# Running sums in a pooling mixer, a fifth pair of weight tiles, and weight units prepared three ahead

## The chip, the core and the metric

The kernel runs on one core of a Trainium2 chip. A core has a matmul engine (TensorE, PE in the profile; PEld is its weight load), a vector engine (DVE), a scalar engine (ACT), a general engine (POOL) and a sync engine (SP) that here issues DMAs. Each takes its instructions in order from a queue of its own and waits on semaphores. They share an on-chip memory (SBUF); matmuls write to eight PSUM banks, which DVE and ACT read. The metric is the device time of one execution in microseconds (us).

## The reference, cut to what matters

A two-layer decoder trunk on 512 tokens of 1,024 channels, all in float32. Each layer has a mixer, cross-attention into 256 memory tokens, and a gated feed-forward (FFN) with a short causal convolution, each behind an RMSNorm. Layer 0's mixer is a gated DeltaNet beside a state-space model; layer 1's is the pooling mixer:

```python
POOL_WINDOWS = (2, 4, 8, 16)             # one per group of 256 channels
for gi, win in enumerate(POOL_WINDOWS):
    csg = cs[..., sl]                    # running sum over the tokens
    lower = jnp.pad(csg, ((0, 0), (win, 0), (0, 0)))[:, 1:t + 1]
    mean = (csg[:, 1:] - lower) / jnp.minimum(pos_count, float(win))
    outs.append(jnp.einsum('btc,ce->bte', mean - xf[..., sl], pool_w[gi]))
return jnp.concatenate(outs, axis=-1) * pool_scale
```

The first tokens, which have fewer than `win` tokens behind them, are divided by their own count.

## The kernel before, in words

Activations lie transposed: eight tiles `x[0..7]` of 128 channels by 512 tokens. Every float32 product is three matmuls of a split into a high and a low half (`mm3`, lines 185 to 187): high by high, low by high, high by low.

**Weight units.** All weights come in a list of units of 128 x 1,024 (512 KB, some 128 x 768), in the order in which PE uses them. A unit is loaded by SP into one of three `raw` tiles (`_load`, line 127), ACT casts it to the high half `wh` (line 136), and the low half `wl` is made in one of two ways: DVE subtracts (line 141), or, for the units listed in `pool_units`, ACT writes minus the raw weights (line 138) and POOL has a DMA add the weights from memory on top (line 139). There are four pairs of `wh` and `wl`. `w()` hands out the next unit and, before that, prepares units up to `LOOK` = 2 ahead. So the cast of unit j has to wait until PE is done with unit j-4, and a raw load until the casts of the unit three before are done.

**Order.** PE and SP run in the order of the code. DVE, ACT and POOL are put in order by the framework's scheduler when the program is built, so their queues are fixed in the program but not written in the code.

**The stretch that matters here** begins when the FFN of layer 0 ends. `pool_mixer` multiplies the normalized tiles by the pool weights (two units, eight products `pl`) and keeps PE going with work in the background, `run(bg, 3)`: the values of layer 1 (`values`, two pairs of products `vp`, eight units, each pair read by `vh` on ACT, line 373, and `vl` on DVE, line 374) and the last five keys (`keys`, products `kp`, five units). Every second of these units gets its low half by DMA. Then the query products of the attention follow (`Q`, products `in`, units `wq`), 24 matmuls of 512 columns each. In the built program the first query product has the PSUM bank of the first value product, and the second that of the third.

Meanwhile DVE takes the windows in the order 8, 16, 4, 2. For each it multiplies the two products by the row of norms (line 646), forms the window sums by doubling adds over 2 x 512 columns (line 649: three for window 8, four for 16, two for 4, one for 2), corrects the first columns by count (653), turns sums into mean minus token (657), and adds the scaled result to the two `x` tiles (660). ACT then makes `xh` and the squares of the new tiles (226, 242), DVE `xl` (227).

Of the kernel before, what the change touches and what calls it, by code (L numbers as in the profile page):

```python
# [14 lines left out]
F32R = mybir.dt.float32r  # L15
I32 = mybir.dt.int32
AF = mybir.ActivationFunctionType
ALU = mybir.AluOpType
# [4 lines left out]
KT = D // 128  # L23
# [33 lines left out]
class Net:  # L57
    def __init__(self, tc, A, ctx):
        self.tc, self.nc, self.A = tc, tc.nc, A
        nc = self.nc  # L60
        P = lambda name, bufs, **k: ctx.enter_context(tc.tile_pool(name=name, bufs=bufs, **k))
        self.cp = P("cp", 1)
        self.wp = P("wp", 1)
        self.ap_ = P("ap", 56)
        self.sc = None
        self.tp = P("tp", 8)
        self.zp = P("zp", 4)
        self.rp = P("rp", 2)
        self.dp = P("dp", 4, space=bass.MemoryType.DRAM)
        self.n = 0  # L70
        self.units = []
        self.pool_units = ()
        self.area = None
        self.tset = "n"
        self.prepped = {}
        self.loaded = {}
        self.ui = 0
        self.small = self.cp.tile([128, NSMALL], F32, name="small")
        o, w = SMALL["g_mix"]
        nc.scalar.dma_start(self.small[:, o : o + w], A["small"][:, o : o + w])  # L80
        self.ident = self.cp.tile([128, 128], F32, name="ident")
        make_identity(nc, self.ident)
        self.ones = self.cp.tile([128, 128], F32, name="ones")
        nc.gpsimd.memset(self.ones, 1.0)
# [33 lines left out]


    LOOK = 2  # L120
    PAD = 8

    def _load(self, i):
        if i not in self.loaded:
# [4 lines left out]
    def _prep(self, i):  # L129
        nc = self.nc  # L130
        self._load(i)
        raw = self.loaded[i]
        n = raw.shape[1]
        H = self.wp.tile([128, n], F32R, tag="wh", bufs=4, name=self.nm("wh"))
        L = self.wp.tile([128, n], F32R, tag="wl", bufs=4, name=self.nm("wl"))
        nc.scalar.copy(H, raw)  # L136
        if i in self.pool_units:
            nc.scalar.activation(L, raw, AF.Copy, scale=-1.0)  # L138
            nc.gpsimd.dma_start(L, self.units[i], accum_op=ALU.add)
        else:  # L140
            nc.vector.tensor_tensor(L, raw, H.bitcast(F32), ALU.subtract)  # L141
        self.prepped[i] = (H, L)

    def first(self, N, src):
# [8 lines left out]
        def part(i, p):  # L153
            nc.sync.dma_start(self.loaded[i][:, p], self.units[i][:, p])
            H, L = self.prepped[i]
            nc.scalar.copy(H[:, p], self.loaded[i][:, p])
            nc.vector.tensor_tensor(L[:, p], self.loaded[i][:, p], H[:, p].bitcast(F32), ALU.subtract)

# [452 lines left out]
    def pool_mixer(self, x, N, bg, after):  # L611
        nc = self.nc
        ws = [self.w(), self.w()]

        for t in self.wb:
            nc.gpsimd.memset(t[:, :, : self.PAD], 0.0)

        def mm(m):
            gi, e = m // 2, m % 2
            w = ws[gi // 2]  # L620
            ps = self.psum("pl")
            for kk in range(2):
                o = (gi % 2) * 512 + kk * 256 + e * 128
                self.mm3(ps, (w[0][:, o : o + 128], w[1][:, o : o + 128]), N["hl"][gi * 2 + kk], kk == 0, kk == 1)
            return ps

        pss = {}
        order = (4, 5, 6, 7, 2, 3, 0, 1)
        for i, m in enumerate(order):
            if i == 4:  # L630
                r = self.norm_end(N)
            pss[m] = mm(m)
            if i >= 4:
                z = self.t(F32, "plz")
                nc.scalar.copy(z, pss[m])
                pss[m] = z
        rB = self.row(r, range(4))

        v = nc.vector
        defer = []  # L640
        for gi in (2, 3, 1, 0):
            win = WINDOWS[gi]
            at = lambda t, sh: t[:, :, self.PAD - sh : self.PAD - sh + T]
            z, ping, pong = self.wb
            for e in range(2):
                v.tensor_tensor(at(z, 0)[:, e, :], pss[2 * gi + e], rB, ALU.mult)
            cur, sh = z, 1
            while sh < win:
                v.tensor_tensor(at(ping, 0), at(cur, 0), at(cur, sh), ALU.add)
                cur, ping, pong = ping, pong, ping  # L650
                sh *= 2
            cur = at(cur, 0)
            v.tensor_tensor(cur[:, :, : win - 1], cur[:, :, : win - 1], self.cnt[:, gi : gi + 1, : win - 1].to_broadcast([128, 2, win - 1]), ALU.mult)
            for f in defer:
                f()
            defer = []
            v.scalar_tensor_tensor(cur, cur, 1.0 / win, at(z, 0), ALU.mult, ALU.subtract)
            for e in range(2):
                m = 2 * gi + e
                v.scalar_tensor_tensor(x[m], cur[:, e, :], self.sm("pool_scale", m), x[m], ALU.mult, ALU.add)  # L660
                after(m, defer)
            self.run(bg, 3)
        for f in defer:
            f()
# [786 lines left out]
def trunk(tc, A, out, ctx):  # L1451
    n = Net(tc, A, ctx)
# [5 lines left out]
    b = 0  # L1458
# [29 lines left out]
    psum = dict(space=bass.MemoryType.PSUM)  # L1488
    with tc.tile_pool(name="mp", bufs=1) as n.mp, tc.tile_pool(name="mix", bufs=1) as n.pp, tc.tile_pool(name="ps", bufs=6, **psum) as n.ps, tc.tile_pool(name="px", bufs=1, **psum) as n.px:
# [6 lines left out]
        x = []  # L1496
        hl = n.mixer0(N, kv, x)
        N = n.norm_begin("g_xa", 0)
        for _ in n.proj_residual(x, hl, lambda m: n.norm_tile(N, x[m]), 3, (4, 6, 7, 8)):
            pass  # L1500
    with tc.tile_pool(name="win", bufs=1) as wpool, tc.tile_pool(name="ps8", bufs=8, **psum) as n.ps:
        for l in range(2):
            if l == 1:
                N = n.norm_begin("g_xa", 1)
                bg = chain(n.values(kv[1], kv[2]), kv[3])
                n.wb = [wpool.tile([128, 2, n.PAD + T], F32, name=n.nm("wb")) for _ in range(3)]
                n.pool_mixer(x, Nn, bg, lambda m, q: n.norm_tile(N, x[m], at=m, defer=q))
                n.run(bg)
            Nf = n.norm_begin("g_ffn", l)
            n.attention(x, N, kv, lambda m: n.norm_tile(Nf, x[m]))  # L1510
            Nn = n.norm_begin("g_final", 0) if l else n.norm_begin("g_mix", 1)
            def next_keys():
                kv[:2] = [], []
                kv.append(n.keys(kv[0], kv[2]))
                n.run(kv[3], 6)

            n.ffn(l, x, Nf, None if l else next_keys, (Nn, out) if l else lambda m: n.norm_tile(Nn, x[m]))
# [73 lines left out]
```

## Time and profile before

| | us |
|---|---|
| median of three runs | 1413.93 (1413.61 to 1413.98) |
| the profiled execution | 1411.4 |
| its span, first to last instruction | 1409.6 |
| PE busy in it | 1356.5 (96%) |
| DVE busy | 909.8 (65%) |
| ACT busy | 618.6 (44%) |
| POOL busy | 220.4 (16%) |

An engine's busy share is an average over stages. What decides is PE's idle time: where it lies, and what ended it. The granted clock of PE (PEclk) is a share of full speed. The first 320 us are the mixer of layer 0, the stretch above runs from about 860 to 930.

### The profile page before, as it was taken

How to read it: one execution, taken by the hardware profiler on the slowest of the kernel's cores; microseconds unless marked ns; L12 is line 12 of the kernel's file. 1: busy time of each engine (PE TensorE's matmuls, PEld its weight loads, DVE VectorE, ACT ScalarE, POOL GpSimd, SP SyncE). 2: the span in 40 equal slices, each digit the busy share in tenths (PEclk: the TensorE clock that was granted, in tenths of full speed). 3: DMA queues.
4: the chain of work that ended last, by engine and by line, in shares of the span. 5: the costliest groups of instructions: out<-in, count | busy, mean ns of one | idle time of the engine just before them, and what ended most of it. 6: DMA issues, size and time to landing. Idle time of an engine off the chain costs nothing.

```text
span 1409.6 us, 17658 instructions
## 1 busy us (share of the span) xinstructions
PE 1356.5 (96%) x6699; PEld 1143.3 (81%) x6699; DVE 909.8 (65%) x1552; ACT 618.6 (44%) x948; POOL 220.4 (16%) x350
## 2 busy tenths in 40 slices
PE   8799988999999999999999999899999999999997
PEld 6678878988788888888888888778888888888886
DVE  7967877466645677637754766965657736663764
ACT  6446574545443444324422445654434423432442
POOL 2495827210200200000000002200100000000003
PEclk9789979999999999999999999989999999999999
DMA  7424424453321323332323236932233333323221
GB/s 233 111 90 105 126 43 124 106 179 106 121 73 46 105 90 105 90 105 90 105 90 102 89 109 149 252 84 64 65 97 98 95 100 93 102 77 118 87 69 69
DMA packets 50628, 146.63 MB, mean 104 GB/s; under 512 B 7664, under 2 KB 13936, under 8 KB 50544
## 3 DMA queue, kind: packets, MB, share of 16 engines
q1 hardware_dynamic: 40480, 127.29, 28.6%
q0 software_dynamic: 3744, 13.63, 5.6%
q10 hardware_dynamic: 6320, 4.60, 1.1%
q8 instruction: 52, 0.85, 0.2%
q14 instruction: 32, 0.26, 0.1%
HBM read 141.30 MB, written 4.19 MB: 103 GB/s over the span
## 4 chain that ended last, share of the span: by engine, by line
PE 80%; DVE 6%; POOL 4%; DMA 3%; ACT 3%; issue 2%; ACTq 1%; POOLq 0%; SPq 0%; DVEq 0%
PE in L185 14%; PE in L186 14%; PE in L187 14%; PE op L186 9%; PE op L185 9%; PE op L187 9%; DVE cv L755 1%; ACT wl L138 1%; DMA so<-dy 1%; DMA dy<-sg 1%; PE kp L186 1%; PE kp L187 1%; PE kp L185 1%; DMA wl<-in_wk 1%; PE sc L187 1%
## 5 line engine op out<-in xcount | busy, mean ns | idle before, releaser
L136 ACT CAST wh<-raw 128x1024 fp32r<-128x1024 f32 (+1 forms) x230 | 237.0, 1036 | 399.7 <-PE op L186 148.0
L185 PE MATMUL in<-xh,wh 128*128 128x512 f32 x992 | 392.2, 395 | 13.9 <-DVE vl L374 7.0
L186 PE MATMUL in<-xl,wh 128*128 128x512 f32 x992 | 389.9, 393 | 0.0
L187 PE MATMUL in<-xh,wl 128*128 128x512 f32 x992 | 389.2, 392 | 0.6 <-DVE wl L141 0.6
L141 DVE TENSOR_TENSOR wl<-raw,wh 128x1024 fp32r<-128x1024 f32 (+1 forms) x204 | 246.1, 1209 | 80.2 <-ACT wh L136 77.9
L185 PEld LDWEIGHTS in<-xh,wh 128*128 128x128 f32 x992 | 188.4, 190 | 53.6 <-DVE vl L374 7.2
L187 PEld LDWEIGHTS in<-xh,wl 128*128 128x128 f32 x992 | 188.3, 190 | 40.5 <-DVE wl L141 1.0
L186 PEld LDWEIGHTS in<-xl,wh 128*128 128x128 f32 x992 | 188.4, 190 | 39.2 <-DVE xl L227 1.0
L247 POOL TENSOR_TENSOR sq<-sq,sq 128x512 f32<-128x512 f32 x28 | 46.7, 1669 | 967.9 <-ACT sq L242 869.5
L469 DVE TENSOR_TENSOR x<-op,x 128x512 f32<-128x512 f32 x68 | 46.9, 690 | 151.2 <-PE op L187 151.2
L185 PE MATMUL op<-fh,wh 128*128 128x512 f32 (+1 forms) x376 | 141.4, 376 | 0.0
L186 PE MATMUL op<-fl,wh 128*128 128x512 f32 (+1 forms) x376 | 141.2, 376 | 0.0
L187 PE MATMUL op<-fh,wl 128*128 128x512 f32 (+1 forms) x376 | 141.2, 376 | 0.0
L572 DVE TENSOR_TENSOR h<-in,rB 128x512 f32<-128x512 f32 x88 | 60.2, 688 | 87.1 <-PE in L187 87.1
L185 PEld LDWEIGHTS op<-fh,wh 128*128 128x128 f32 x376 | 70.8, 188 | 12.9
L186 PEld LDWEIGHTS op<-fl,wh 128*128 128x128 f32 x376 | 70.8, 188 | 12.7
L187 PEld LDWEIGHTS op<-fh,wl 128*128 128x128 f32 x376 | 70.8, 188 | 12.7
L192 ACT CAST fh<-a 128x512 fp32r<-128x512 f32 x44 | 27.3, 621 | 110.6 <-DVE a L584 110.6
L576 ACT ACTIVATE a<-h,small 128x512 f32<-128x512 f32 x88 | 63.3, 721 | 10.5 <-DVE h L572 9.8
L578 DVE SCALAR_TENSOR_TENSOR a<-h,small,a 128x510 f32<-128x510 f32 x88 | 65.8, 750 | 2.9
L577 DVE SCALAR_TENSOR_TENSOR a<-h,small,a 128x511 f32<-128x511 f32 x88 | 65.4, 746 | 2.5 <-ACT a L576 2.5
L580 ACT ACTIVATE a<-a 128x512 f32<-128x512 f32 x44 | 27.8, 632 | 81.0 <-DVE a L578 81.0
(460 smaller groups left out, 2111.7 us busy)
## 6 DMA issues: line engine op xcount, KB each, us to landing
raw<-in_up SPq DMA_DIRECT2D x88, 512.0 KB, 3.5
raw<-in_dn SPq DMA_DIRECT2D x32, 512.0 KB, 3.5
raw<-in_w_in SPq DMA_DIRECT2D x18, 512.0 KB, 4.3
raw<-in_wk SPq DMA_DIRECT2D x16, 512.0 KB, 4.4
raw<-in_wv SPq DMA_DIRECT2D x16, 512.0 KB, 3.9
raw<-in_wq SPq DMA_DIRECT2D x16, 512.0 KB, 4.5
raw<-in_wo SPq DMA_DIRECT2D x16, 512.0 KB, 3.5
raw<-in_dn SPq DMA_DIRECT2D x16, 384.0 KB, 2.9
```

The costliest lines, as they stand in the source:

```text
L136: nc.scalar.copy(H, raw)
L141: nc.vector.tensor_tensor(L, raw, H.bitcast(F32), ALU.subtract)
L185: mm(ps, wh, xh, start=start, stop=False)
L186: mm(ps, wh, xl, start=False, stop=False)
L187: mm(ps, wl, xh, start=False, stop=stop)
L247: eng.tensor_tensor(N["acc"], N["acc"], sq, ALU.add)
L469: nc.vector.tensor_tensor(x[m], ps, x[m], ALU.add)
L572: nc.vector.tensor_tensor(h, ps, rB, ALU.mult)
L576: nc.scalar.activation(a, h, AF.Copy, scale=cw(2))
L577: nc.vector.scalar_tensor_tensor(a[:, 1:], h[:, : T - 1], cw(1), a[:, 1:], ALU.mult, ALU.add)
L578: nc.vector.scalar_tensor_tensor(a[:, 2:], h[:, : T - 2], cw(0), a[:, 2:], ALU.mult, ALU.add)
L580: nc.scalar.activation(a, a, AF.Silu)
```

## The change

It has three parts. Window sums: for windows 8 and 16 DVE keeps a running sum with one scan per tile (add the new column, subtract the one `win` back), which needs 16 columns of zeros ahead of the tile (`PAD`); window 4 keeps its two adds; window 2 becomes half of the token before minus the token, with the half put into the scale (`half`, made once). Weights: when the first mixer is over, every fifth unit has a pair of its own in a new pool `wx`, so five pairs rotate. And from there on `LOOK` is 3.

```diff
-    PAD = 8
+    PAD = 16
...
     def _prep(self, i):
...
-        H = self.wp.tile([128, n], F32R, tag="wh", bufs=4, name=self.nm("wh"))
-        L = self.wp.tile([128, n], F32R, tag="wl", bufs=4, name=self.nm("wl"))
+        p, b = (self.wx, 1) if self.wx and i % 5 == 4 else (self.wp, 4)
+        H = p.tile([128, n], F32R, tag="wh", bufs=b, name=self.nm("wh"))
+        L = p.tile([128, n], F32R, tag="wl", bufs=b, name=self.nm("wl"))
...
     def pool_mixer(self, x, N, bg, after):
...
+        half = self.tiny(KT, "half")
+        v.tensor_scalar_mul(half, self.sm("pool_scale", 0, KT), 0.5)
...
-            cur, sh = z, 1
-            while sh < win:
-                v.tensor_tensor(at(ping, 0), at(cur, 0), at(cur, sh), ALU.add)
-                cur, ping, pong = ping, pong, ping
-                sh *= 2
-            cur = at(cur, 0)
-            v.tensor_tensor(cur[:, :, : win - 1], cur[:, :, : win - 1], self.cnt[:, gi : gi + 1, : win - 1].to_broadcast([128, 2, win - 1]), ALU.mult)
+            z0 = at(z, 0)
+            cur = at(ping, 0)
+            scale = lambda m: self.sm("pool_scale", m)
+            if win == 2:
+
+                v.tensor_tensor(cur, at(z, 1), z0, ALU.subtract)
+                v.memset(cur[:, :, 0:1], 0.0)
+                scale = lambda m: half[:, m : m + 1]
+            else:
+                if win == 4:
+                    v.tensor_tensor(at(pong, 0), z0, at(z, 1), ALU.add)
+                    v.tensor_tensor(cur, at(pong, 0), at(pong, 2), ALU.add)
+                else:
+
+                    for e in range(2):
+                        v.tensor_tensor_scan(cur[:, e, :], z0[:, e, :], at(z, win)[:, e, :], 0.0, ALU.add, ALU.subtract)
+                v.tensor_tensor(cur[:, :, : win - 1], cur[:, :, : win - 1], self.cnt[:, gi : gi + 1, : win - 1].to_broadcast([128, 2, win - 1]), ALU.mult)
...
-            v.scalar_tensor_tensor(cur, cur, 1.0 / win, at(z, 0), ALU.mult, ALU.subtract)
+            if win > 2:
+                v.scalar_tensor_tensor(cur, cur, 1.0 / win, z0, ALU.mult, ALU.subtract)
...
-                v.scalar_tensor_tensor(x[m], cur[:, e, :], self.sm("pool_scale", m), x[m], ALU.mult, ALU.add)
+                v.scalar_tensor_tensor(x[m], cur[:, e, :], scale(m), x[m], ALU.mult, ALU.add)
...
-    with tc.tile_pool(name="win", bufs=1) as wpool, tc.tile_pool(name="ps8", bufs=8, **psum) as n.ps:
+    with tc.tile_pool(name="win", bufs=1) as wpool, tc.tile_pool(name="wx", bufs=1) as n.wx, tc.tile_pool(name="ps8", bufs=8, **psum) as n.ps:
+        n.LOOK = 3
```

The orders of PE and SP stay as they were. On ACT, at the end of the background work, the queue before reads (`raw_1503`, `raw_1508`, `raw_1521` are the second, third and fourth query units, `x_583` and `x_584` are tiles 2 and 3 of `x`, `vp_1427` is the first value product):

```order
L136 CAST wh_1504_8015<-raw_1503_8013 128x1024
L138 ACTIVATE wl_1505_8016<-raw_1503_8013 128x1024
L136 CAST wh_1509_8051<-raw_1508_8049 128x1024
L136 CAST wh_1522_8111<-raw_1521_8109 128x1024
L138 ACTIVATE wl_1523_8112<-raw_1521_8109 128x1024
L226 ACTIVATE xh_1444_7723<-x_583_3154,small_75 128x512
L242 ACTIVATE sq_1446_7726<-x_583_3154 128x512
L226 ACTIVATE xh_1447_7730<-x_584_3156,small_75 128x512
L242 ACTIVATE sq_1449_7733<-x_584_3156 128x512
L373 ACTIVATE vh_1453_7754<-vp_1427_7632,r_406_2305 128x512
L373 ACTIVATE vh_1455_7758<-vp_1428_7633,r_406_2305 128x512
```

There the two `vh` are behind the casts of three query units. Now, at the same place on ACT (`raw_1496`, `raw_1500`, `raw_1507`, `raw_1512` are the first to fourth query units, `vp_1431` the first value product; lines are those of the changed code):

```order
L138 CAST wh_1497_7951<-raw_1496_7949 128x1024
L349 CAST kh_1336_7239<-kt_1335_7238 128x256
L228 ACTIVATE xh_1448_7731<-x_583_3154,small_75 128x512
L244 ACTIVATE sq_1450_7734<-x_583_3154 128x512
L228 ACTIVATE xh_1451_7738<-x_584_3156,small_75 128x512
L244 ACTIVATE sq_1453_7741<-x_584_3156 128x512
L375 ACTIVATE vh_1457_7763<-vp_1431_7643,r_406_2305 128x512
L138 CAST wh_1501_7985<-raw_1500_7983 128x1024
L140 ACTIVATE wl_1502_7986<-raw_1500_7983 128x1024
L375 ACTIVATE vh_1459_7767<-vp_1432_7644,r_406_2305 128x512
L138 CAST wh_1508_8023<-raw_1507_8021 128x1024
L138 CAST wh_1513_8058<-raw_1512_8056 128x1024
```

The first `vh` now stands ahead of the second query unit's cast, the second ahead of the third's. A little further on ACT, the `vh` of the second pair of value products (`vp_1461`) stands behind the cast of the fifth query unit (`raw_1525`):

```order
L244 ACTIVATE sq_1468_7795<-x_581_3150 128x512
L140 ACTIVATE wl_1514_8059<-raw_1512_8056 128x1024
L228 ACTIVATE xh_1469_7799<-x_582_3152,small_75 128x512
L244 ACTIVATE sq_1471_7802<-x_582_3152 128x512
L138 CAST wh_1526_8119<-raw_1525_8117 128x1024
L375 ACTIVATE vh_1481_7869<-vp_1461_7771,r_406_2305 128x512
L375 ACTIVATE vh_1483_7873<-vp_1462_7772,r_406_2305 128x512
```

Before, the casts of that unit came after this `vh`. On DVE, the window of 16 read before:

```order
L646 TENSOR_TENSOR wb_1391_7498<-pl_1403_7538,rB_1420_7610 128x512
L227 SCALAR_TENSOR_TENSOR xl_1422_7621<-x_585_3158,small_75,xh_1421_7620 128x512
L649 TENSOR_TENSOR wb_1392_7499<-wb_1391_7498 128x2x512
L141 TENSOR_TENSOR wl_1470_7807<-raw_1468_7804,wh_1469_7806 128x1024
L227 SCALAR_TENSOR_TENSOR xl_1425_7627<-x_586_3160,small_75,xh_1424_7626 128x512
L649 TENSOR_TENSOR wb_1393_7500<-wb_1392_7499 128x2x512
L141 TENSOR_TENSOR wl_1476_7846<-raw_1474_7843,wh_1475_7845 128x1024
L649 TENSOR_TENSOR wb_1392_7499<-wb_1393_7500 128x2x512
L649 TENSOR_TENSOR wb_1393_7500<-wb_1392_7499 128x2x512
L653 TENSOR_TENSOR wb_1393_7500<-wb_1393_7500,cnt_98 128x2x15
```

and now (line 666 is the scan, printed under the name of a like operation, twice in a row):

```order
L650 TENSOR_TENSOR wb_1394_7508<-pl_1406_7548,rB_1423_7620 128x512
L229 SCALAR_TENSOR_TENSOR xl_1426_7632<-x_585_3158,small_75,xh_1425_7631 128x512
L666 SCALAR_TENSOR_TENSOR wb_1395_7509<-wb_1394_7508 128x512 x2
L143 TENSOR_TENSOR wl_1465_7776<-raw_1463_7773,wh_1464_7775 128x1024
L229 SCALAR_TENSOR_TENSOR xl_1429_7638<-x_586_3160,small_75,xh_1428_7637 128x512
L667 TENSOR_TENSOR wb_1395_7509<-wb_1395_7509,cnt_98 128x2x15
```

Four adds have become two scans, and one weight subtract that stood between them has moved behind.

## Rows read from the trace of the kernel before

**Rows 1.** The page, part 1: busy us, share of the span, count.

```profile
PE 1356.5 (96%) x6699; PEld 1143.3 (81%) x6699; DVE 909.8 (65%) x1552; ACT 618.6 (44%) x948; POOL 220.4 (16%) x350
```

**Rows 2.** Windows: length, busy us and count by engine, clock, DMA share, GB/s.

```profile
860.00:920.00 60.00, 50.77 (x278) 43.15 (x277) 48.63 (x66) 36.69 (x47) 14.81 (x13) 0.96 0.87 219
920.00:980.00 60.00, 60.00 (x299) 50.92 (x298) 37.50 (x81) 27.99 (x57) 0.00 (x0) 0.96 0.23 69
```

**Rows 3.** Timeline of PE: start, us, instruction, idle before it and its releaser.

```profile
890.28 0.50 PE L186 MATMUL vp<-wl,mz 128*128 128x512 f32 x1 [0.80 <-DMA wl<-in_wv]
...
896.62 0.39 PE L187 MATMUL kp<-mz,wl 128*128 128x256 f32 x1 [0.46 <-DMA wl<-in_wk]
...
909.20 0.38 PE L187 MATMUL kp<-mz,wl 128*128 128x256 f32 x1 [1.00 <-DMA wl<-in_wk]
...
918.92 0.79 PE L185 MATMUL in<-xh,wh 128*128 128x512 f32 x1 [6.96 <-DVE vl L374]
```

**Rows 4.** Windows within the stretch, columns as in rows 2.

```profile
858.00:872.00 14.00, 14.00 (x66) 11.54 (x65) 7.07 (x19) 7.69 (x12) 1.74 (x2) 1.00 0.68 159
872.00:880.00 8.00, 8.00 (x39) 6.50 (x37) 6.92 (x7) 4.90 (x6) 0.86 (x1) 1.00 0.69 151
880.00:896.00 16.00, 15.20 (x66) 11.95 (x64) 14.36 (x17) 10.38 (x13) 5.00 (x4) 1.00 1.00 251
896.00:912.00 16.00, 14.50 (x120) 13.94 (x118) 15.36 (x18) 9.58 (x12) 4.71 (x4) 1.00 0.92 238
912.00:918.90 6.90, 0.00 (x0) 0.00 (x0) 4.74 (x8) 5.41 (x8) 3.15 (x3) 0.69 0.95 260
918.90:925.00 6.10, 6.08 (x14) 4.79 (x15) 6.10 (x10) 3.52 (x6) 0.23 (x1) 0.51 0.50 103
```

**Rows 5.** Timeline of ACT in the stretch.

```profile
880.66 1.06 ACT L138 ACTIVATE wl<-raw 128x1024 fp32r<-128x1024 f32 x1 [1.51 <-PE vp L186]
...
913.24 1.04 ACT L136 CAST wh<-raw 128x1024 fp32r<-128x1024 f32 x1 [4.28 <-DMA raw<-in_wq]
...
915.15 0.71 ACT L226 ACTIVATE xh<-x,small 128x512 fp32r<-128x512 f32 x1
...
917.42 1.24 ACT L373 ACTIVATE vh<-vp,r 128x512 fp32r<-128x512 f32 x2
```

**Rows 6.** Transfers: POOL's issue; the chain of waits; the load issued at 908.0.

```profile
882.01 0.86 POOL L139 DMA_DIRECT2D wl<-in_wv  x1 [4.74 <-ACT wl L138]
...
907.13 6.01 DMA raw<-in_wq
...
L127 SPq DMA_DIRECT2D raw<-in_wq x1: 328/328/328, 908.0 to 908.0; - x1
...
DMA to landing us min/median/max: 8.2/8.2/8.2
```

**Rows 7.** Timeline of DVE in the stretch.

```profile
875.36 3.75 DVE L649 TENSOR_TENSOR wb<-wb 128x1024 f32<-128x1024 f32 x3
...
907.93 0.41 DVE L348 TENSOR_TENSOR kl<-kt,kh 128x256 fp32r<-128x256 f32 x1
...
909.60 1.22 DVE L141 TENSOR_TENSOR wl<-raw,wh 128x1024 fp32r<-128x1024 f32 x1
910.73 1.41 DVE L660 SCALAR_TENSOR_TENSOR x<-wb,small,x 128x512 f32<-128x512 f32 x2
...
914.84 1.23 DVE L657 SCALAR_TENSOR_TENSOR wb<-wb,wb 128x1024 f32<-128x1024 f32 x1
918.12 0.75 DVE L374 SCALAR_TENSOR_TENSOR vl<-vp,r,vh 128x512 fp32r<-128x512 f32 x1 [2.06 <-ACT vh L373]
```

**Rows 8.** Scans of the first mixer: ns min/median/max of one; four in the chain.

```profile
L1412 DVE TENSOR_TENSOR_SCAN sz<-m,sz x16: 391/394/1496, 118.5 to 290.1; 128x128 f32<-128x128 f32 x16
...
219.53 1.28 DVE sz L1412 x4
```

**Rows 9.** Timeline of DVE: a small row beside the place of the new one.

```profile
14.21 0.16 DVE L842 COPY ein<-small 128x4 f32<-128x4 f32 x1
```

More of the change, by code (lines that the diff above doesn't have):

```diff
@@ L72, in __init__ @@
         self.pool_units = ()
+        self.wx = None
         self.area = None
```

## The prediction

> **What bounds the kernel now.** I read the page's busy shares first: PE is busy 96% of the span [rows 1]. Then the windows by stage, to find where the rest is. From the end of the first mixer to the tail PE fills its windows, as in 920 to 980, except in 860 to 920, where 50.77 of 60 us are busy [rows 2]: the pooling mixer of layer 1 with the values and keys of its attention. The change can win there, or in what it moves elsewhere; where PE is full, ACT or DVE time saved gives nothing.
>
> PE's timeline shows the 9.23 us: waits of 0.80, 0.46, 1.00 and 6.96 us [rows 3]. The first three end on "DMA wl<-in_wv" or "wl<-in_wk": low halves that POOL has a DMA add up. The long one ends on DVE vl, the low half of the first value tile: the first query group takes the PSUM bank of that value product and cannot start while the bank is unread. The windows show a second loss: while PE idles (912 to 918.9) the granted clock falls to 0.69, and in the next 6.1 us it is 0.51, the 1.2 GHz level, where it was 1.00 from 858 to 912 [rows 4]. In those 6.08 busy us stand 14 matmuls; at full clock one of 512 columns takes 0.23 (66 in 15.20 us of 880 to 896), 14 take 3.2. So 2.9 us go to the clock. **Together 12.1 us, the most that this stretch can return.**
>
> Behind the long wait stands ACT's order: its cast at 913.24 had waited 4.28 us for raw<-in_wq, the fourth query unit's, which was asked for at 907.13 and took 6.01 us; vh comes behind that cast, at 917.42 [rows 5, 6]. DVE then sat 2.06 us until vh [rows 7].
>
> **The fifth pair and the third unit ahead.** With four pairs the cast of unit j waits for PE's last matmul on unit j-4; now unit j+1 stands at that place of the queue and waits for unit (j+1)-5, the same one. So in the steady stages (attention, FFN) each wait stays where it is, and PE, already full, gains nothing: 0, bounds 0 and 0. PE's and SP's orders are unchanged. Only where units are used up faster than they are made does the depth count.
>
> (a) *The three short waits.* One of them reads: PE releases the pair, ACT's wl runs 880.66 to 881.72, POOL issues at 882.01, PE has the data at 890.28 [rows 3, 5, 6]: 9.6 us. A unit holds PE here for 12 matmuls of 512 columns (or 24 of 256) at 0.23 us a 512, 2.8 us. Four pairs give three units of notice, 8.4 us; 1.2 are missing (the wait was 0.80). Five pairs give 11.2, 1.6 to spare. The three waits, 2.26 us, go, unless the DMAs take longer: their share is 1.00 in 880 to 896 and 0.92 in 896 to 912, but 0.68 and 0.69 in 858 to 880 [rows 4]. There 0.32 x 14 + 0.31 x 8 = 7.0 us of DMA time lie idle, which a unit fetched earlier can use. I take 0.9 us as still waited for, somewhat nearer to none than to all; bounds 0 and 2.3.
>
> (b) *The long wait.* In ACT's new order the first vh stands behind the work on tiles 2 and 3 but ahead of the casts of the second, third and fourth query units; the raw that was late no longer stands in front of it. What is late next is the latest of three: PE itself, whose keys end at 918.92 - 6.96 = 911.96 [rows 3], less the 2.26 of (a), 909.7; ACT, which needs x of tiles 2 and 3 from DVE; and DVE. The next part gives 909.9 for these. So 0.2 to 0.3 us stay of 6.96, and without a long idle time the 2.9 us of half clock go too. Bounds: 0, and 1.5 should the scans be dear.
>
> (c) *The next wait.* The second query group takes a bank of the second pair of value products, whose vh and vl now stand behind the casts of the fourth and fifth query units. The fifth's raw was asked for at 908.0 and landed 8.2 us later, at 916.2 [rows 6]. It goes out one unit (2.8 us) earlier, and (a) takes up to 2.3 off as well: 911.1 to 913.4. Behind it come a cast (1.0), DVE's subtract of that unit (1.2) and vl (0.75), so the bank is free at 914.1 to 916.4; the first query group, 24 matmuls from 909.9, and four short transposes end at about 915.8. Waited: 0 to 0.6; 3.4 if the landing stays at 916.2. I take 0.9.
>
> **The running sums.** A doubling add of 2x512 columns costs 1.25 us (3.75 for three [rows 7]). Window 8 loses three, window 16 four: 8.7 us. Each gets two scans of 512 columns. The trace has scans of 128 columns only: four in a row take 1.28 us, 0.32 each [rows 8]. Four times that counts the fixed part four times: 1.28, the upper end; 0.69, a little over half an add, would be a scan at an add's rate, the lower. I take 1.1: 0.32 less some 0.06 that is fixed is 2.0 ns a column, twice the add's slope, and that row is a scan's own. Four: 4.5 us, bounds 2.8 and 5.1. Window 4 keeps its two adds. Window 2 loses the count row and the step of 1.23 us [rows 7], and gets a subtract for its add and a small memset: some 1.3 less, none of it ahead of x of tiles 2 and 3. Ahead of these, DVE's order also has two weight subtracts fewer (1.2 each) and no key step (0.41), which stand behind them now. So x of these tiles, ready at 910.73 + 1.41 = 912.1, comes at 912.1 - (8.7 - 4.5) - 2.8 = 905.1, all of DVE's waits kept. ACT then needs two xh and two squares (915.15 to 917.42 in rows 5, 2.3) and vh 0.6: 908.0. DVE does two products (1.3, about an add), a weight subtract (1.2), the key step (0.4) and window 2's subtract (1.2) to 909.2, and vl to 909.9. DVE was busy 14.36 and 15.36 of 16 us in the two windows before 912 [rows 4], so the time saved is needed.
>
> **Small parts.** The halved scale is one more DVE row of 8 columns in the first mixer, among such of 0.16 us [rows 9]: 0.1, bounds 0 and 0.2. The wider zero margins are three POOL memsets far ahead of their use: 0.
>
> **Sum.** 12.1 - 0.9 - 0.3 - 0.9 - 0.1 = 9.9 us. The profiled execution took 1411.4 (span 1409.6), 2.5 under the median of 1413.93; I take the gain off the median: **1404.0**. With the bounds of (a) to (c) and of the scans: 1401.9 to 1405.2.
>
> **Rivals.** *DMA is the limit.* If the DMA engines, full from 880 on, deliver no earlier, the waits of (a) stay, keys end at 912.0, the first query group ends at 918.1, and the fifth query unit's raw at 916.2 frees the bank at 919.2. Still lost: 2.3 + 0.3 + 1.1, and up to 2 for what the deeper fetching takes from transfers that are due sooner: a gain of 6.4 to 8.4, 1405.5 to 1407.5. For it: share 1.00 at 251 GB/s; against it: the 7.0 us idle before [rows 4]. The Trainium skill has the rule on "DMA: Bandwidth & Descriptors", section "Issuing engines are not separate DMA queues": transfers started from SP, ACT and POOL end up on the same 16 engines and interleave. By it the extra unit's two transfers can come only out of idle time; the trace has such time. Chance 0.14.
>
> *The clock falls in short waits too.* If one or two waits of (a) and (c) each bring a half-clock stretch of 2.9 us, the gain is 4.1 to 7.0: 1406.9 to 1409.8. Against it: the waits of 0.46 to 1.00 us fell in windows of clock 1.00 [rows 3, 4]; only the 6.96 us did it. The Trainium skill describes such a case on "TensorE: Matmul & The Clock Gate", section "A second HAM failure mode: psum-queue depth-cycling": frequent brief idling between groups of matmuls made the clock swing. This trace, with three brief waits, does not show it. Chance 0.07.
>
> *Slower: the scans.* The slowest of the 16 scans took 1.50 us for 128 columns [rows 8]. At that rate one of 512 takes 6.0, four take 19.6 more than I count: x of tiles 2 and 3 at 924.7, the first query group at 929.5, 10.6 later than now, about 1424. It turns to a loss where a scan passes 3.4 us (905.1 + 4(S - 1.1) + 4.8 = 918.9). Against it: the median is 0.39. Chance 0.04.
>
> *It does nothing.* Another wait of the same size fills the gap: within 0.2%, 1411.1 to 1416.7. Against it: the place of vh has changed in the program itself. Chance 0.05.
>
> **How the numbers follow.** Forecast 0.70. 0.2% (2.8 us), about what a measurement can tell from no change, bounds "same". Faster: 0.70 + 0.14 + 0.07 = 0.91; same 0.05; slower 0.04. The range takes in the forecast and the DMA rival: 1401.5 to 1407.5.
>
> **What would show it.** Right: PE busy some 58 of 60 us in 860 to 920, no wait over 1.5 us, clock 1.00 there and behind; scans of 512 columns at 1.1 to 1.2 us; the first query matmul some 9 us earlier; windows before 860 the same, those after 980 only shifted. Wrong: a wait of several us that ends on a bank or a raw in the same place, a half-clock stretch, scans of several us, or a changed first 320 us.

## The result, and the profile after

The changed kernel took 1407.2 us (median of 6 runs, 1404.0 to 1409.6), the kernel before 1414.0 beside it. The ratio on record, over all runs, is 0.9936, 95% interval 0.9917 to 0.9956; that of the two medians alone is 0.9952. A second set gave 1407.7 against 1413.3, 0.9965 (0.9954 to 0.9977). So it is faster; the medians differ by 6.8 and 5.6 us. The first set lies inside the predicted range, 0.3 us below its upper end, and the second 0.2 above it. Forecast were 9.9 us, 1404.0.

To see where, I cut the span at three matmuls of PE's timeline: layer 0's first query matmul, the first pooling matmul, the first score matmul of layer 1. In the profiled execution (1406.27 us):

```profile
378.46 0.47 PE L187 MATMUL in<-xh,wh 128*128 128x512 f32 x1 [0.88 <-ACT wh L138]
...
861.64 0.39 PE L187 MATMUL pl<-xh,wh 128*128 128x512 f32 x1
...
932.91 0.28 PE L187 MATMUL sc<-kh,qh 128*128 128x256 f32 x1
```

| part of the span, us | before | after | moved |
|---|---|---|---|
| first mixer, to 378 | 378.15 | 378.46 | +0.31 |
| middle: layer 0's attention and FFN | 482.32 | 483.18 | +0.86 |
| stretch: pooling, values, keys, first queries | 78.19 | 71.27 | -6.92 |
| tail: from the first score matmul | 470.93 | 471.54 | +0.61 |
| span | 1409.59 | 1404.45 | -5.14 |

The stretch is where the gain is, as forecast. Two windows by stage, as [rows 2], and two within the stretch, as [rows 4] (length, busy us by engine, clock, DMA share, GB/s):

```profile
860.00:920.00 60.00, 57.22 (x304) 47.56 (x303) 48.95 (x70) 39.56 (x52) 17.30 (x13) 1.00 0.80 194
920.00:980.00 60.00, 58.86 (x306) 50.07 (x306) 36.45 (x78) 27.19 (x55) 0.00 (x0) 1.00 0.32 94
...
912.00:918.00 6.00, 4.56 (x19) 3.06 (x17) 6.00 (x7) 5.80 (x8) 3.38 (x4) 1.00 0.83 171
918.00:925.00 7.00, 5.39 (x23) 3.82 (x24) 6.03 (x11) 2.83 (x6) 0.00 (x0) 1.00 1.01 269
```

PE is busy 57.2 of 60 us (50.8 before), and the clock stays at 1.00 throughout. What PE still waits for, by its timeline, as [rows 3]:

```profile
902.73 0.38 PE L189 MATMUL kp<-mz,wl 128*128 128x256 f32 x1 [0.73 <-DMA wl<-in_wk]
...
915.71 0.50 PE L188 MATMUL in<-xl,wh 128*128 128x512 f32 x1 [0.82 <-DVE xl L229]
...
918.17 0.50 PE L188 MATMUL in<-xl,wh 128*128 128x512 f32 x1 [0.79 <-DVE xl L229]
...
919.44 0.50 PE L188 MATMUL in<-xl,wh 128*128 128x512 f32 x1 [0.30 <-DVE xl L229]
...
921.84 0.50 PE L187 MATMUL in<-xh,wh 128*128 128x512 f32 x1 [1.14 <-DVE vl L376]
```

The wait of 6.96 us is gone: the first query group starts at 911.64, right behind the keys. Of the short waits on low halves one of 0.73 is left (and one of 0.1). New are the three waits on xl, the low halves of the attention's own input, which the prediction's sum did not have. DVE's timeline, as [rows 7], shows it at work from 874 to 923 but for one pause, with some instructions at twice their usual length:

```profile
876.48 2.33 DVE L666 TENSOR_TENSOR_SCAN wb<-wb 128x512 f32<-128x512 f32 x2
...
884.49 3.39 DVE L666 TENSOR_TENSOR_SCAN wb<-wb 128x512 f32<-128x512 f32 x2
887.81 1.19 DVE L143 TENSOR_TENSOR wl<-raw,wh 128x1024 fp32r<-128x1024 f32 x1
...
897.15 0.75 DVE L229 SCALAR_TENSOR_TENSOR xl<-x,small,xh 128x512 fp32r<-128x512 f32 x1 [2.46 <-ACT xh L228]
897.82 2.34 DVE L661 TENSOR_TENSOR wb<-wb 128x1024 f32<-128x1024 f32 x1
...
901.78 1.21 DVE L662 TENSOR_TENSOR wb<-wb 128x1024 f32<-128x1024 f32 x1
...
905.71 1.41 DVE L675 SCALAR_TENSOR_TENSOR x<-wb,small,x 128x512 f32<-128x512 f32 x2
...
910.85 0.74 DVE L376 SCALAR_TENSOR_TENSOR vl<-vp,r,vh 128x512 fp32r<-128x512 f32 x1
...
911.65 2.68 DVE L675 SCALAR_TENSOR_TENSOR x<-wb,half,x 128x512 f32<-128x512 f32 x2
...
919.91 1.21 DVE L143 TENSOR_TENSOR wl<-raw,wh 128x1024 fp32r<-128x1024 f32 x1
921.04 1.40 DVE L376 SCALAR_TENSOR_TENSOR vl<-vp,r,vh 128x512 fp32r<-128x512 f32 x2
```

Two scans of 512 columns take 2.33 us, 1.17 each, where 1.1 was taken; the second pair took 3.39. L661 and L662 are the same add, 2.34 and 1.21. The short ones ran alone, the long ones beside a GpSimd add of squares. The pause, 2.46 us, was for an xh of ACT, and ACT had stood for a raw, as in [rows 5]:

```profile
894.49 1.06 ACT L140 ACTIVATE wl<-raw 128x1024 fp32r<-128x1024 f32 x1 [3.62 <-DMA raw<-in_wk]
```

### The profile page after: what moved, and what is told of

The parts are those of the page before. It is cut to its first block, busy times and chain, and to the rows that moved or that the text cites. A ratio compares the mean times of both kernels' runs of the same rounds, so it can differ in the third digit from the quotient of the medians.

```text
span 1404.5 us, 17657 instructions
## 1 busy us (share of the span) xinstructions
PE 1356.5 (97%) x6699; PEld 1141.8 (81%) x6699; DVE 903.7 (64%) x1549; ACT 617.9 (44%) x948; POOL 222.7 (16%) x350
## 4 chain that ended last, share of the span: by engine, by line
PE 80%; DVE 8%; ACT 4%; issue 2%; DMA 2%; POOL 2%; ACTq 0%; POOLq 0%; SPq 0%; DVEq 0%
PE in L187 15%; PE in L188 15%; PE in L189 14%; PE op L188 9%; PE op L187 9%; PE op L189 9%; DVE cv L770 1%; DVE wl L143 1%; DMA so<-dy 1%; DMA dy<-sg 1%; PE sc L189 1%; PE sc L188 1%; PE sc L187 1%; PE pv L187 1%; PE pv L189 1%
## 5 line engine op out<-in xcount | busy, mean ns | idle before, releaser
L187 PE MATMUL in<-xh,wh 128*128 128x512 f32 x992 | 390.9, 394 | 8.1 <-ACT xh L228 5.7
L188 PE MATMUL in<-xl,wh 128*128 128x512 f32 x992 | 389.3, 392 | 1.9 <-DVE xl L229 1.9
L189 PE MATMUL in<-xh,wl 128*128 128x512 f32 x992 | 388.0, 391 | 0.5 <-DVE wl L143 0.5
L187 PEld LDWEIGHTS in<-xh,wh 128*128 128x128 f32 x992 | 187.5, 189 | 48.5 <-ACT xh L228 6.3
L188 PEld LDWEIGHTS in<-xl,wh 128*128 128x128 f32 x992 | 187.4, 189 | 42.2 <-DVE xl L229 4.2
L189 PEld LDWEIGHTS in<-xh,wl 128*128 128x128 f32 x992 | 187.3, 189 | 40.5 <-DVE wl L143 1.0
L187 PE MATMUL op<-fh,wh 128*128 128x512 f32 (+1 forms) x376 | 141.5, 376 | 0.0
L188 PE MATMUL op<-fl,wh 128*128 128x512 f32 (+1 forms) x376 | 141.5, 376 | 0.0
L189 PE MATMUL op<-fh,wl 128*128 128x512 f32 (+1 forms) x376 | 141.1, 375 | 0.0
L574 DVE TENSOR_TENSOR h<-in,rB 128x512 f32<-128x512 f32 x88 | 60.2, 688 | 88.3 <-PE in L189 88.3
L187 PEld LDWEIGHTS op<-fh,wh 128*128 128x128 f32 x376 | 70.7, 188 | 13.2
L189 PEld LDWEIGHTS op<-fh,wl 128*128 128x128 f32 x376 | 70.7, 188 | 13.0
L188 PEld LDWEIGHTS op<-fl,wh 128*128 128x128 f32 x376 | 70.7, 188 | 12.7
```

Source lines behind the costliest of these rows:

```text
L187: mm(ps, wh, xh, start=start, stop=False)
L188: mm(ps, wh, xl, start=False, stop=False)
L189: mm(ps, wl, xh, start=False, stop=stop)
L574: nc.vector.tensor_tensor(h, ps, rB, ALU.mult)
```

## Experiments

Times are ratios to the kernel before, run on the same chip beside each. The first mixer's length differs from execution to execution (layer 0's first query matmul came between 377.5 and 382.3 us in 14 profiled executions), so I judge by the other three parts too. In "ss later" the transposes of layer 1's sum of squares stand one query group further back; "+64 B" is the fifth pair 64 bytes higher.

| kernel | ratio (95%) or time | middle | stretch | tail |
|---|---|---|---|---|
| before | 1 | 482.32 | 78.19 | 470.93 |
| changed | 0.9936 (0.9917-0.9956) | 483.18 | 71.27 | 471.54 |
| changed again | 0.9965 (0.9954-0.9977) | 483.15 | 72.14 | 471.54 |
| pair and depth alone | 1.0004 (0.9990-1.0017) | 483.16 | 76.19 | 471.79 |
| sums alone | 0.9950 (0.9935-0.9965) | 482.34 | 72.19 | 471.12 |
| no GpSimd adds | 0.9945 (0.9927-0.9963) | 483.20 | 69.92 | 472.46 |
| no accumulating DMAs | 0.9951 (0.9938-0.9965) | 483.15 | 69.48 | 471.80 |
| pair 12.7 KB lower | 1413.0, one run | 485.12 | 72.33 | 473.81 |
| pair 12.7 KB lower, +64 B | 1411.6, one run | 484.56 | 72.41 | 473.25 |
| pair +64 B, first execution | 1405.1, one run | 482.30 | 70.89 | 471.12 |
| pair +64 B | 0.9957 (0.9942-0.9971) | 482.31 | 71.71 | 471.13 |
| pair in the stretch only | 0.9943 (0.9928-0.9958) | 482.31 | 72.59 | 471.13 |
| the same, ss later | 0.9939 (0.9922-0.9957) | 482.31 | 71.45 | 471.13 |
| pair +64 B, ss later | 0.9947 (0.9933-0.9961) | 482.32 | 70.94 | 471.15 |

**The two halves of the change apart.** Pair and depth alone: the changed kernel with the old doubling adds.

```diff
-                    for e in range(2):
-                        v.tensor_tensor_scan(cur[:, e, :], z0[:, e, :], at(z, win)[:, e, :], 0.0, ALU.add, ALU.subtract)
...
+            while sh < win:
+                v.tensor_tensor(at(ping, 0), at(cur, 0), at(cur, sh), ALU.add)
...
```

> The fifth pair and three units ahead alone, with the old doubling adds. I judge by the stretch from the first pooling matmul to the first score matmul (PE's work in it is the same in all kernels): 78.2 us before, 71.3 in the changed kernel. Theory (the sums free the first bank, the pair only shortens the waits on low halves): DVE's chain to x of tiles 2 and 3 is 4.2 us longer again (8.7 of doubling adds instead of 4.5 of scans), so the first query group waits 4 to 6 us for the first vl, with the clock low for a while behind it; the short waits are at most 0.9 together. Stretch 75 to 78, time 1409 to 1413. Rival (the new place of vh in ACT's queue comes from the depth): stretch 71 to 73, time 1406 to 1408.

Sums alone: no fifth pair, two units ahead.

```diff
-    with tc.tile_pool(name="win", bufs=1) as wpool, tc.tile_pool(name="wx", bufs=1) as n.wx, ...
-        n.LOOK = 3
+    with tc.tile_pool(name="win", bufs=1) as wpool, ...
```

Without that pool `self.wx` stays empty, and `_prep` takes the four pairs for every unit.

> The running sums alone, with four pairs and two units ahead. Theory: the long wait on the first vl is gone (under 1 us) and the clock stays at 1.00, but PE still waits for DMA-made low halves, 2.3 us together, about 1.5 more than in the changed kernel: stretch 72 to 74, time 1.5 above the changed kernel. Rival 1 (the DMA engines are the limit, so a unit fetched earlier brings nothing): waits on low halves as in the changed kernel, 0.8, stretch 71.3, same time as the changed kernel. Rival 2 (depth does it): the long wait of several us stays, stretch above 75.

PE's timeline of the first, then of the second:

```profile
910.01 0.39 PE L189 MATMUL kp<-mz,wl 128*128 128x256 f32 x1 [2.89 <-DMA wl<-in_wk]
...
917.57 0.79 PE L187 MATMUL in<-xh,wh 128*128 128x512 f32 x1 [4.70 <-DVE vl L376]
```

```profile
894.44 0.50 PE L188 MATMUL vp<-wl,mz 128*128 128x512 f32 x1 [2.48 <-DMA wl<-in_wv]
...
908.31 0.39 PE L189 MATMUL kp<-mz,wl 128*128 128x256 f32 x1 [2.34 <-DMA wl<-in_wk]
```

With the pair and the depth alone the long wait stays, 4.70 us, and no time is gained. The sums alone remove it and gain as much as the whole change: middle, stretch and tail add up to 1025.7 us, in the changed kernel to 1026.0 and, in a second execution, 1026.8. So the running sums free the first bank. Three details failed. The pair shortens the waits on low halves only beside the sums (4.8 us of them without it, 0.8 and 2.3 with it): beside the old adds 2.89 are left, where at most 0.9 were expected and the kernel before had 2.26. With the sums alone these waits were 4.8 and not 2.3 us, and the time was not above the changed kernel's. And the clock did not stay at 1.00: behind the wait of 2.34 us it fell, in the window

```profile
910.00:913.00 3.00, 3.00 (x16) 3.00 (x16) 2.52 (x4) 2.58 (x4) 1.28 (x1) 0.50 1.01 213
```

**The changed kernel again.**

> The changed kernel once more, unchanged, for the spread of its time and of its stages. Its runs so far lie between 1404.0 and 1409.6, and outside the pooling stretch its profiled execution was 1.6 us slower than that of before, spread evenly as 0.2% longer matmul distances. Theory (that is the execution, not the kernel): the stretch is again 71.3 within 0.3, and the rest of the span differs from run to run by 1 to 3 us. Rival (the changed kernel is slower elsewhere by its own doing): the rest is again 1.6 us longer than in the kernel before.

The theory fell: the stretch was 0.9 us longer this time, while the middle and the tail came out the same to 0.03 us, 1.5 us longer than before. So the changed kernel is slower there by its own doing. In the FFN, 24 matmuls of a unit take 5.440 us, but every fifth unit 5.494, in this execution, in the first profile and in every kernel whose fifth pair lies where the changed kernel's does. Groups of PE by line for such two units, one behind the other (busy, mean ns of one):

```profile
L189 PE MATMUL in<-xh,wl 128*128 128x512 f32 x9 | 3.5, 390 | 0.0
L188 PE MATMUL in<-xl,wh 128*128 128x512 f32 x8 | 3.1, 390 | 0.0
L187 PE MATMUL in<-xh,wh 128*128 128x512 f32 x8 | 3.1, 389 | 0.0
```

```profile
L189 PE MATMUL in<-xh,wl 128*128 128x512 f32 x9 | 3.5, 389 | 0.0
L188 PE MATMUL in<-xl,wh 128*128 128x512 f32 x8 | 3.2, 395 | 0.0
L187 PE MATMUL in<-xh,wh 128*128 128x512 f32 x8 | 3.1, 392 | 0.0
```

No wait is shown; the matmuls with the high half of that pair (L187, L188) are themselves 3 to 5 ns longer, those with its low half (L189) are not. Three kernels with the same instructions in the same order, and the pair elsewhere, asked whether it is the place: the first with the pools swapped (byte 207488 of a partition in the built program instead of 220160), the second with a gap of 64 bytes (220224), the third with both (207552):

```diff
-    with tc.tile_pool(name="win", bufs=1) as wpool, tc.tile_pool(name="wx", bufs=1) as n.wx, ...
+    with tc.tile_pool(name="wx", bufs=1) as n.wx, tc.tile_pool(name="win", bufs=1) as wpool, ...
+        n.wx.tile([128, 16], F32, name="gap")
```

> The changed kernel with the fifth pair placed ahead of the pooling buffers in SBUF, 12.7 KB lower (offset 207488 in a partition instead of 220160), with the same order of instructions. In the changed kernel every fifth unit of the steady stages (the one whose weights lie in the fifth pair) takes 5.494 us for its 24 matmuls, the others 5.440: 0.054 a unit, about 1.4 us over the program; before, all take 5.440. Theory A (it is where the pair lies, high in the partition): here the fifth unit takes 5.440 too. Theory B (it is not the place, but that the pair is a separate one, or its casts come at another moment): 5.494 stays.

> The changed kernel with the fifth pair moved up by 64 bytes (220224 instead of 220160), so that it stands to a 128-byte grid as the other four pairs do (they start 64 bytes off it). Theory C (the 0.054 us a unit is a matter of alignment): the fifth unit takes 5.440 us. Otherwise 5.494.

> The fifth pair ahead of the pooling buffers as in the run where its units took 5.598 us, but 64 bytes higher (offset 207552 instead of 207488). Theory (it is the 64 bytes, the grid on which the pair stands against the other tiles, not the height in the partition): units of the fifth pair take 5.440 us as all others. Rival (it is the place, and 220224 was a good one): over 5.47.

12.7 KB lower the unit takes 5.60 us, which neither theory had, read from the starts of the first matmuls of three units in a row (the second is the fifth pair's):

```profile
527.93 0.39 PE L187 MATMUL in<-xh,wh 128*128 128x512 f32 x1
...
533.37 0.40 PE L187 MATMUL in<-xh,wh 128*128 128x512 f32 x1
...
538.97 0.39 PE L187 MATMUL in<-xh,wh 128*128 128x512 f32 x1
```

64 bytes higher than in the changed kernel it takes 5.440, as the others (groups by line, that unit):

```profile
L189 PE MATMUL in<-xh,wl 128*128 128x512 f32 x9 | 3.5, 389 | 0.0
L187 PE MATMUL in<-xh,wh 128*128 128x512 f32 x8 | 3.1, 389 | 0.0
L188 PE MATMUL in<-xl,wh 128*128 128x512 f32 x8 | 3.1, 389 | 0.0
```

So it is the place. It is not height (lower was worse), and not the 64 bytes alone: at 207552 the unit still took 5.589. Which property of the address counts stays open. The longer run of the pair 64 bytes higher:

> The changed kernel with its fifth pair 64 bytes higher, again, with its time. Theory (the tax of 0.054 us on each unit of the fifth pair is gone, about 1.4 us over the program, and the stretch is the changed kernel's): 1.0 to 2.0 us below the changed kernel, median 1405 to 1406.5, from the first query matmul of layer 0 to the first pooling matmul 482.3. Rival (one lucky execution): same as the changed kernel, 1407.4.

Middle and tail fall by 0.87 and 0.41 us, so the place cost 1.3 us. Its median (1407.4) shows none of it, against the expectation. The first mixer scatters by more than that: in this profile layer 0's first query matmul came at 382.3 us, 3.9 later than in the first of the changed kernel, and the single first execution of the same kernel took 1405.1.

**What is left in the stretch.** Two kernels leave out work. Without the GpSimd adds:

```diff
+            if N.get("skip") and k < 6:
+                return
             eng = nc.gpsimd if k < 6 and not N["quick"] else nc.vector
```

> The changed kernel without the five GpSimd adds of squares in layer 1's pooling mixer (the norm of the attention there sums three of eight tiles, so its output differs). Theory (DVE's instructions beside a GpSimd add take about twice as long, and DVE's lateness is what PE still waits for): a pair of scans takes 2.3 us each time instead of 3.39 once, the first add of window 4 1.2 instead of 2.34, the steps of x 1.4 a pair instead of 2.68; the three waits on xl (1.91) and the one on the second vl (1.14) lose 2 of their 3 us: stretch 69 to 70, time 1.5 to 2.5 below the changed kernel. Rival (order, not speed: xl stands behind other work whatever its speed; or the late raw sets the time): waits on xl stay, stretch 71 to 71.5, same time.

DVE's timeline there, against 3.39, 2.34 and 2.68 above, and PE's waits:

```profile
883.99 2.33 DVE L668 TENSOR_TENSOR_SCAN wb<-wb 128x512 f32<-128x512 f32 x2
...
898.65 1.22 DVE L663 TENSOR_TENSOR wb<-wb 128x1024 f32<-128x1024 f32 x1
...
910.33 1.42 DVE L677 SCALAR_TENSOR_TENSOR x<-wb,half,x 128x512 f32<-128x512 f32 x2
```

```profile
903.61 0.46 PE L189 MATMUL kp<-mz,wl 128*128 128x256 f32 x1 [2.12 <-DMA wl<-in_wk]
...
920.02 0.50 PE L187 MATMUL in<-xh,wh 128*128 128x512 f32 x1 [0.46 <-DVE vl L378]
```

Each of the three is 1.1 to 1.3 us shorter: DVE's slowness there is the GpSimd adds, shown. The stretch is 69.9. The second query group starts 58.9 us behind the first pooling matmul, where it was 60.2 in the changed kernel, and these 1.3 us are the whole difference. The waits on xl are gone too, but that proves less: PE also came later, by a wait on a low half of 2.12 us and half clock behind it (0.53 from 903.6 to 907.2). The tail is 0.9 us longer, 0.25 of it a wait at its start; the rest I have not followed. The Trainium skill has the rule on "SBUF — State Buffer", section "Who interferes with whom": a DVE instruction with two SBUF inputs contends with a GpSimd instruction that reads SBUF, and the pair of ports that they share is an exclusive lock. The rows agree: the excess is about one GpSimd add (1.30 us alone). The prediction lacked this, though the kernel before shows it, on two adds of one line and on POOL:

```profile
901.04 1.22 DVE L649 TENSOR_TENSOR wb<-wb 128x1024 f32<-128x1024 f32 x1
...
904.56 2.32 DVE L649 TENSOR_TENSOR wb<-wb 128x1024 f32<-128x1024 f32 x1
```

```profile
902.74 3.06 POOL L247 TENSOR_TENSOR sq<-sq,sq 128x512 f32<-128x512 f32 x2
```

Up to x of tiles 2 and 3 such rows cost DVE 2.8 us before and 3.2 after. Most of the loss is thus old; new are the 1.3 on the steps of x behind it.

Without the accumulating DMAs:

```diff
+            if i not in self.plain:
                 nc.gpsimd.dma_start(L, self.units[i], accum_op=ALU.add)
```

> The changed kernel without the accumulating DMAs of the nine low halves that the pooling stretch makes that way (those weights' low halves are the negated raw values, so the output differs): 4.5 MB less to move between about 865 and 925 us, nothing else left out. Theory (what is left in the stretch is two things of like size, the low halves that land late and DVE's lateness): PE's waits on wl (0.8 in the first profiled execution, 2.6 in the second) go to 0, ACT's wait of 3.6 us for a raw falls under 1, x of tiles 2 and 3 comes about 2 us earlier: stretch 68 to 70 (changed kernel 71.3 and 72.1). Rival 1 (the DMA engines are not what limits): stretch 71 to 72. Rival 2 (they are all of it): waits on xl and on the bank go too, stretch 66 to 67.

The waits on low halves go (in the second execution they were 2.3 us by its rows, not 2.6), a wait on DVE stays, and the stretch is 69.5: neither rival. The second query group starts 58.4 us behind the first pooling matmul, 1.8 earlier than in the changed kernel, which again is the whole difference. Timelines of PE and ACT there, and two windows, the second at half clock behind the wait:

```profile
917.12 0.50 PE L190 MATMUL in<-xl,wh 128*128 128x512 f32 x1 [1.87 <-DVE xl L231]
```

```profile
894.74 1.06 ACT L141 ACTIVATE wl<-raw 128x1024 fp32r<-128x1024 f32 x1 [3.92 <-DMA raw<-in_wk]
```

```profile
880.00:896.00 16.00, 16.00 (x70) 12.92 (x69) 15.89 (x19) 9.54 (x12) 1.31 (x1) 1.00 0.48 148
...
919.00:922.00 3.00, 2.95 (x10) 2.12 (x8) 3.00 (x5) 1.97 (x3) 0.00 (x0) 0.56 0.25 104
```

One expectation failed: ACT still waited 3.92 us for that raw, with the DMA engines half idle (share 0.48). That raw landed 3.6 us after its issue (5.4 and 6.3 in the two executions of the changed kernel), so transfers do lengthen each other; but it went out late. SP's waits in the changed kernel from 872 to 912 say why (engine, line, what it waited for: us, times, longest):

```profile
SPq L128 <- DVE wl L143: 15.5, 3, 7.5
```

The fetch waits for one of three raw buffers, and the buffer for a subtract that stands behind the scans on DVE: the one of 887.81 in DVE's rows above, and the fetch went out at 889.0, when it ended. DVE's lateness thus comes back as a late raw, which holds up ACT, and DVE again.

**Better placed.** The fifth pair for the three units of the stretch alone, and, in two kernels, layer 1's sum-of-squares transposes behind the second query group:

```diff
-        p, b = (self.wx, 1) if self.wx and i % 5 == 4 else (self.wp, 4)
+        p, b = (self.wx, 1) if self.wx and i in self.fifth else (self.wp, 4)
-            if u == 0:
+            if u == (1 if self.wb else 0):
                 r = self.norm_end(N)
```

> The changed kernel, but the fifth pair serves only three units, those of the pooling stretch (the 5th, 10th and 15th unit of layer 1), and four pairs serve all others. Theory (the pair costs 0.054 us for each unit that uses it, some 35 of them, and gains 0 to 1 us in the stretch): all steady units 5.440; from the first query matmul of layer 0 to the first pooling matmul 482.3 us as before (changed kernel: 483.2); stretch 71 to 72; time about 1.4 below the changed kernel, 1405 to 1406. Rival (the pair gains nothing in the stretch, or the tax is a matter of three units ahead): stretch 72 to 73, or 483.2 stays; time as the changed kernel.

> As the run with the fifth pair in the stretch alone, and in layer 1 the transposes of the sum of squares stand behind the second query group instead of the first (the scale they give is first needed by the first scores' softmax). Theory (PE reaches them before the last two adds of squares are done, and stands still for what DVE has queued): stretch 0 to 1 us shorter, 70 to 71.5. Rival (what PE waits for are xl and the bank, these come first anyway): same stretch; or the softmax starts later and PE waits at the first probabilities' transposes, up to 1 us longer behind the stretch.

> The fifth pair 64 bytes higher, and layer 1's transposes of the sum of squares behind the second query group. Theory (behind the first query group PE waited 1.1 us for a bank that the second vl frees late; with the transposes later, that bank is another, freed earlier, and DVE's adds of squares are off the path): stretch 69.5 to 70.5 where the changed kernel had 71.3 and 72.1; time 2.5 to 3.5 below the changed kernel. Rival (the wait on DVE only moves to the next place in PE's order): same as the run with the pair 64 bytes higher alone.

In all three the middle is back at 482.3. The stretch is another matter. With the pair in the stretch alone it grew to 72.6: ACT's order came out otherwise, a cast waited 6.57 us for raw<-in_wq ahead of vh, and the wait on the first bank is back:

```profile
914.02 0.79 PE L188 MATMUL in<-xh,wh 128*128 128x512 f32 x1 [3.07 <-DVE vl L377]
```

With the pair 64 bytes higher and the later transposes the wait on the second bank is gone, the three on xl stay (0.85, 0.79, 0.30), and the stretch is 70.94, against 71.71 and 70.89 with the transposes in place: at most 0.8, less than expected. Its three parts sum to 1024.4 us, those of the changed kernel to 1026.0 and 1026.8 (1025.2 and 1024.3 with the transposes in place). With the pair in the stretch alone they sum to 1026.0, with the later transposes too to 1024.9. So by their parts three of the four kernels are 0.8 to 2.5 us below the changed one, of which the pair's place is 1.3, and the pair in the stretch alone is level with it: what it saves outside it loses inside. The times do not show it: three medians are 1405.0 to 1405.3, but the kernel before ran at 1412.0 and 1413.4 beside them, and the ratios lie among those of the changed kernel. I cannot rank the four.

## Why the prediction was right and where it failed

**The bound and (b): right, with the wrong parent.** The stretch was where time could be won; the long wait and the half clock went. The stretch began 1.2 us later in this profile (861.64 against 860.47); with that taken off, x of tiles 2 and 3 was ready at 905.9 (905.1 forecast) and vl ended at 910.4 (909.9). The first query matmul stood 0.3 us for it, as taken. But (b) stood under the fifth pair and the third unit. The halves apart show that the place of vh follows from the running sums.

**The fifth pair elsewhere: wrong.** "0, bounds 0 and 0" counted the order only. The place of the pair in SBUF lengthened its matmuls: 1.3 us. No row of before could show it; a new buffer's bounds should not have been 0 and 0.

**(a): the size by luck.** 0.9 was to remain; 0.8 did in the first profile, 2.3 in the second. The argument was notice against time needed (11.2 against 9.6 us), with idle DMA time to be used. The DMA shares in 858 to 880, 0.77 and 0.70 where they were 0.68 and 0.69, used 1.3 of those 7.0 us. The step left out the raw buffers. Counted from the start of the stretch, the last value unit and the first two keys were fetched 1.5 to 2.8 us earlier than before, but the third key, whose fetch waited for DVE's subtract, 0.5 us later.

**(c): the step that was mis-sized.** The wait at the second bank was 0.9 by forecast and 1.14 by trace, and this is luck. The bank was to be free at 914.1 to 916.4; its vl ran from 921.04 (919.9 in the time of before), behind a weight subtract. The fetch of the fifth query unit, which was to go out a unit earlier, went out at 911.4, 2.3 us later than before by the same count. PE came late as well, because the sum followed only vh and vl and had nothing for the xl that the first query group needs in its second half: 1.91 us of waits. Had PE not stood there, it would have stood at the bank: from the second query group's start to the first score matmul it needs 11.1 us in both executions and in both kernels that leave out work, so this start sets the end of the stretch. Behind it is DVE. Its four scans took 5.7 us where 4.5 were taken (four at 1.1 are 4.4), 1.1 of it beside a GpSimd add; the steps of x lost 1.3 the same way; and it stood 2.46 for ACT's xh, behind the late raw, which "all of DVE's waits kept" did not foresee. How much each of these weighs by itself is not shown.

**The account.** The stretch was to fall by 10.0 (9.9 and the 0.1 of the small part) and fell by 6.9 and 6.1. Idle time understates a wait. From start to start the wait of 0.79 cost 1.07 us, as 1.19 and 0.34 us passed on its two sides where 0.227 is usual (5.440 over 24):

```profile
916.98 0.40 PE L187 MATMUL in<-xh,wh 128*128 128x512 f32 x1
918.17 0.50 PE L188 MATMUL in<-xl,wh 128*128 128x512 f32 x1 [0.79 <-DVE xl L229]
918.51 0.39 PE L189 MATMUL in<-xh,wl 128*128 128x512 f32 x1
```

Counted so, waits and half clock cost 13.1 us before (12.1 in the prediction) and 5.9 after: 2.7 for xl, 1.5 for the second bank, 1.4 for low halves, 0.3 for the first vl. The difference is 7.2; the stretch of the first profile fell by 6.9. Of the 3.1 that were missed, 2.7 are thus xl, 0.6 the second bank, 0.5 low halves and 0.3 unassigned, less the 1.0 that there was more to win. Middle and tail add 1.5, the first mixer 0.3. So the profiled gain was 5.1 us instead of 9.9.

**The range: luck.** The bounds of (a), (b), (c) and the small part (2.3, 1.5, 3.4, 0.2), all at their worst, leave a gain of 4.7, which is 1409.2 and not 1405.2; how 1405.2 came about is not said. The result lies above 1405.2, and is in the range only through the upper end that the first rival set.

**The rivals.** *DMA is the limit* has the result in its range (1405.5 to 1407.5), by a mechanism that is part of it: without the accumulating DMAs 1.8 to 2.7 us of the stretch go. *The clock falls in short waits* has it too (1406.9 to 1409.8), but did not happen in the changed kernel. In three others waits of 1.87, 2.12 and 2.34 us were each followed by some 3 us at about half clock, while waits of 1.88, 2.27, 2.48 and 2.89 were not: the length of the wait alone does not tell. *The scans slow* was far off: 1.17 us a scan, 3.4 needed.

## What to carry to other kernels

Follow every operand of the group that is to start earlier, not only the one that was last: with the longest wait gone, PE stood for three others and for the next bank, all on DVE. Judge the halves of a change apart: here one gave the gain, and the other paid a little and cost as much. Where runs scatter by several us, compare stages between fixed instructions: those repeated to 0.03 us where no wait was involved. Take a wait from start to start of the instructions around it, not from the idle time shown.

## What the hardware did that I had not expected

The same matmuls took 227 ns apart on four pairs of weight tiles and up to 233 on the fifth, by nothing but its place in SBUF: 24 of them 5.440 us at byte 220224 of a partition, 5.494 at 220160, 5.589 at 207552, 5.598 at 207488. Why is open. And DVE instructions with two SBUF operands lost 1.1 to 1.3 us each beside a GpSimd add that takes 1.3 alone.
